# Half of one dense token tile's gates by scatter, two choices to a column; v block by block into four buffers; 16 early rows

## The chip, the core and the metric

The kernel runs on one core of a Trainium2 chip. The metric is the device time of one execution in microseconds. Before the change it is 1724.55 us, the median of three runs (1724.57, 1723.10, 1724.55).

## What is computed

A decoder layer on 512 tokens (plus 16 learned meta tokens): a state-space branch and an mLSTM branch are merged, and the result goes through PEER, a mixer that picks experts by product keys. The change touches only PEER. Every token has 8 heads; a head picks 16 of 128 x 128 = 16384 experts, each of which is one row of `u_tab` and one of `v_tab`:

```python
def block(xb):
    q = (xb @ w_q).astype(f32).reshape(PEER_TOKEN_BLOCK, PEER_HEADS, 2, PEER_HALF)
    s = jnp.einsum('thid,hikd->thik', q, keys32)
    sv, si = lax.top_k(s, PEER_TOPK)
    ...
    cs, ci = lax.top_k(cand, PEER_TOPK)
    eidx = jnp.take_along_axis(cidx, ci, axis=-1)
    gate = jax.nn.softmax(cs, axis=-1)
    ug = u_tab[eidx]
    act = jax.nn.gelu(jnp.einsum('td,thkd->thk', xb, ug).astype(f32))
    vg = v_tab[eidx]
    return jnp.einsum('thk,thkd->td', (gate * act).astype(vg.dtype), vg)
```

After it the layer's input is added and a last norm is taken.

## The kernel before

Everything up to the PEER queries (`front`) takes about the first 475 us. In `peer` the 512 tokens are four tiles of 128.

**Tile 0 gathers.** Its 128 choices per token are 128 columns. For each column GpSimd fetches 128 rows of u by an indirect DMA (`fetch`), VectorE multiplies with the tokens and sums (`use`, L1142), and later 128 rows of v are fetched and added into `ac0` (L1150). Of these 256 rows `NEARLY` = 25 are fetched before the main loop (tiles `ge`), the rest in it (tiles `g`).

**Tiles 1 to 3 are dense.** The experts are 128 blocks j of 128. `hidden(j)` computes u-block times tokens: 8 x 3 TensorE products (the float32 operand is split by ScalarE and VectorE into a high part `uh` and a low part `ul`, and three of the four partial products are taken, L84, L87 and L88) and a GELU, which gives `act`. In the main loop each block j forms `w` = gates x `act`, splits it (`wh`, `wl`), splits v's block (`vh`, `vl`) and adds 18 products of 128x512 to the three output tiles `o`. Each engine's instructions stand in one order, and each is begun in that order.

**Hidden blocks ahead of the loop.** `NSP` = 44 pairs of blocks (88 blocks) are computed in the stages before the loop, written to DRAM (`ad`) and read back in the loop (`act<-ad`); `LEFT` = 8 blocks are computed last before the loop and stay on chip; the other 32 are computed in the loop, six blocks ahead of their use (`RA`).

**Gates.** Dense gates are a matrix of 16384 experts by 384 tokens, mostly zeros. Tiles 2 and 3 make theirs by one-hot matrices (`gates`): for 8 tokens at a time VectorE builds `o` (L1045, one compare) and `ow` (L1045, one multiply), TensorE multiplies them token by token into `gp` (L1486), ScalarE copies them out to `stg` (L1488), and each 32 tokens are a block of 2 MB that is written to `gd`. Tile 1 scatters: `pairs_of` computes an address for each of the 128 x 128 choices (`ix`), and `scatter` lets GpSimd add one column of 128 gates at a time into `gds`, a DRAM array that `front` has filled with zeros by 8 DMAs. A head's 16 columns follow the head before. The last 32 tokens of tile 3 have their u rows gathered too (`NSIDE` = 32 rows `ge<-in_u,xsi`, L1349 and L1357).

**What sets the order.** In the gate stage `beside` paces GpSimd: six scatters, then three early rows, by a clock that counts TensorE's work; a row's VectorE instruction is put into the program when it is due, `LAG` after its slot. `fill` spreads the hidden blocks over the stage. Tile 1's and 3's pairs and those of tile 0 come first, those of tile 2 beside the gates. The early rows lie in the buffers of v (`vraw`, two of 1 MB, each a pair of blocks). In the loop SyncE's one queue issues all plain loads: v by pairs, u by pairs, `act`, and `gin` (gates of 8 blocks, from `gds` and `gd`). A load waits in that queue until its buffer is free, and what stands behind it waits too.

Of the kernel before, what the change touches and what calls it, by code (L numbers as in the profile page):

```python
# [11 lines left out]
F32 = mybir.dt.float32  # L12
# [3 lines left out]
I32 = mybir.dt.int32  # L16
# [35 lines left out]
JB = 8  # L52
PAR = (("g1", 8), ("a_re", 16), ("a_im", 16), ("log_dt", 16), ("b_glu", 4), ("conv_w", 32), ("conv_b", 8),
# [11 lines left out]
def tile_hybrid_block(ctx: ExitStack, tc: tile.TileContext, a: dict, out: bass.AP, dbg: dict | None = None):  # L65
# [55 lines left out]
    gds = dram.tile([P, NKEY // JB, P // TB, JB, TB], F32, name="gds")  # L121
# [8 lines left out]
def front(tc, a, dbg, cst, dram, xnp, ident, h2d, xsd, gds, x0, qt01, dump, split, mm3, rsqrt, rsqrt_cols):  # L130
# [3 lines left out]
    with es:  # L134
# [63 lines left out]
        blank = [x for x in gds.rearrange("i g b j t -> (i g b j t)").rearrange("(n p c d) -> n p c d", n=8, p=P, d=D)]  # L198
# [825 lines left out]
def peer(tc, a, out, dbg, cst, dram, xh, xl, blanks, ident, h2d, xsd, gds, x0, qt01, dump, split, mm3, rsqrt_cols):  # L1024
# [9 lines left out]
    NSP = 44  # L1034
# [3 lines left out]
    NEARLY = 25  # L1038
# [3 lines left out]
    GS = 32768.0  # L1042

# [4 lines left out]
    with es:  # L1048
# [3 lines left out]
        gd = dram.tile([2 * P // TB, P, NKEY, TB], F32, name="gd")  # L1052
# [175 lines left out]
        def pairs_of(i, h0=0, h1=PH):  # L1228
# [3 lines left out]
            if h0 == 0:  # L1232
                prs[i] = [pw.tile([P, PH, TOPK], F32, tag=t, name=f"{t}{i}") for t in ("cs", "ef")]
                prs[i].append(pool.tile([P, P], F32, name="gw1") if i == 1 else w0 if i == 0 else
                              pw.tile([P, P], F32, tag="gw", name=f"gw{i}"))
                if i == 1:
                    prs[i].append(pool.tile([P, P], I32, name="ix1"))
                if i == NT - 1:
                    prs[i].append(pw.tile([P, P], F32, tag="er", name="er", bufs=1))
# [66 lines left out]
            if i == 1:  # L1306
                ix = prs[i][3].rearrange("p (h k) -> p h k", h=PH)[:, hs]
                off = pw.tile([P, nh, TOPK], F32, tag="off", name=f"off{n_}", bufs=1)
                V.tensor_copy(ix, ef)
                V.tensor_scalar(ix, ix, JB - 1, None, op0=OP.bitwise_and)  # L1310
                V.tensor_copy(off, ix)
                V.tensor_scalar(ef, ef, float(P), cpf[:, 0:1], op0=OP.mult, op1=OP.add)
                V.scalar_tensor_tensor(ef, off, float(TB - P), ef, op0=OP.mult, op1=OP.add)
                V.tensor_copy(ix, ef)
                cols.extend((prs[i][3], prs[i][2], c) for c in range(h0 * TOPK, h1 * TOPK))
# [5 lines left out]
        RB = 3  # L1321
        NE = 6
        C0 = 24
        LAG = 18.0
        early = dict(t=8.0, columns=0, due=[], got=0, used=0, may=0, jk=None, last=None)
# [43 lines left out]
        def beside(flush=False):  # L1369


            e, total = early, NSIDE + NEARLY
            while True:
# [6 lines left out]
                if e["t"] > t or not cols and e["got"] == total:  # L1380
                    break
                n = min(RB, e["may"] - e["got"], NE - (e["got"] - e["used"]))
                if n > 0 and (not cols or e["columns"] % 6 == 0 and e["got"] < (e["columns"] - C0) // 6 * RB):
                    for n in range(e["got"], e["got"] + n):
                        k = n % NE
                        if k < 4:
                            if k % 2 == 0:
                                e["two"] = up.tile([P, 2, D], F32, tag="vraw", name=f"ge{n}", bufs=2)
                            r = e["two"][:, k % 2]
                        else:  # L1390
                            r = rw.tile([P, D], F32, tag=f"early{k}", name=f"ge{n}", bufs=1)
                        e["last"] = tc.keep_in_program_order(fetch_early(n, r))
                        e["t"] += 1.65
                        e["due"].append(e["t"] + LAG + 2.0 * (n % RB))
                        e["got"] += 1
                elif cols:
                    scatter(1)
                    e["t"] += 2.2 if e["columns"] % TOPK else 4.0
                else:
                    break  # L1400

        def scatter(n):

            early["columns"] += len(cols[:n])
            for ix, wt, c in cols[:n]:
# [4 lines left out]
                h = c // TOPK  # L1410
                if c % TOPK == 0:
                    heads.append([])
# [18 lines left out]
        def gates(i, others, blocks):  # L1431
# [33 lines left out]
            for b in blocks:  # L1465
                stg = rw.tile([P, NKEY, TB], F32, tag="stg", name=f"stg{i}{b}")
                for q in range(TB // 8):
# [23 lines left out]
                    fill(1.35 + 0.68 * np_)  # L1491
                    next(others, None)
                    next(others, None)
                SY.dma_start(gd[(i - 2) * (P // TB) + b], stg)
# [16 lines left out]
        whole = 4 * 24 + 2 * 16 * 2.75 + NSIDE * 1.3 + 6  # L1511
# [15 lines left out]
        def beside_gates():  # L1527
            yield from filled(2)

# [13 lines left out]
        for of in ((1, PH // 2, PH), (3,), (0,)):  # L1543
            for _ in filled(*of):
                pass
            if of == (3,):
                placed(prs[NT - 1][3], 3)
                spread()
                early["jk"] = True
                early["may"] = NSIDE  # L1550
            if of == (0,):
                placed(prs[0][1].rearrange("p h k -> p (h k)"), 0)
                V.tensor_copy(e0, prs[0][1].rearrange("p h k -> p (h k)"))
                early["may"] = NSIDE + NEARLY
        rest = beside_gates()
        gates(3, rest, range(P // TB - 1))
        gates(2, rest, range(P // TB))
        assert early["used"] >= NSIDE, early
# [32 lines left out]
        def added(i, c, eng=None):  # L1591

            y, x = hr[i][:, cc[c]], op_[i - 1] if i else ac0
            if sq[i] is None:
                two = up.tile([P, 2, D], F32, tag="vraw", name=f"sq3{i}", bufs=2)
# [173 lines left out]
```

## Time and profile before

| | |
|---|---|
| time, three runs | 1724.57, 1723.10, 1724.55 us |
| profiled execution | 1725.33 us, its span 1723.3 us |
| TensorE | 1634.4 us busy, 95% of the span |
| VectorE, ScalarE, GpSimd | 1307.8, 703.2, 755.3 us busy |
| mean granted TensorE clock | 0.979 |
| bytes moved | 427.51 MB, mean 248 GB/s |

The profile is of one execution. A row of groups gives line, engine, operation, tiles written and read, count, then busy time and mean ns. A row of windows gives the stretch, its length, the busy time (with count) of TensorE's products, its weight loads, VectorE, ScalarE and GpSimd, the granted clock, the DMA engines' busy share and GB/s. A row of waits gives who waited for whom: total, times, longest. Busy time of TensorE counts a product from its start to its modelled end, so products that follow each other overlap; its real pace is read from start to start.

### The profile page before, as it was taken

How to read it: one execution, taken by the hardware profiler on the slowest of the kernel's cores; microseconds unless marked ns; L12 is line 12 of the kernel's file. 1: busy time of each engine (PE TensorE's matmuls, PEld its weight loads, DVE VectorE, ACT ScalarE, POOL GpSimd, SP SyncE). 2: the span in 40 equal slices, each digit the busy share in tenths (PEclk: the TensorE clock that was granted, in tenths of full speed). 3: DMA queues.
4: the chain of work that ended last, by engine and by line, in shares of the span. 5: the costliest groups of instructions: out<-in, count | busy, mean ns of one | idle time of the engine just before them, and what ended most of it. 6: DMA issues, size and time to landing. Idle time of an engine off the chain costs nothing.

```text
span 1723.3 us, 25271 instructions
## 1 busy us (share of the span) xinstructions
PE 1634.4 (95%) x9437; PEld 1426.9 (83%) x9437; DVE 1307.8 (76%) x2621; ACT 703.2 (41%) x1151; POOL 755.3 (44%) x506
## 2 busy tenths in 40 slices
PE   7999999999999999999999939999999989999997
PEld 7898787778889899988999928887888877777785
DVE  6996723366578899885687748887888877887986
ACT  4544454433233244544465613333333423333333
POOL 2000032232132778687887634343335645554640
PEclk9999999999999999999999969999999999999999
DMA  4514353114433367788989899999999989898983
GB/s 174 124 58 102 113 194 123 50 61 161 178 126 131 67 165 246 241 284 281 289 284 303 317 338 364 379 380 371 382 372 383 365 344 346 328 354 329 350 330 136
DMA packets 143427, 427.51 MB, mean 248 GB/s; under 512 B 42020, under 2 KB 58532, under 8 KB 125768
## 3 DMA queue, kind: packets, MB, share of 16 engines
q1 hardware_dynamic: 77048, 267.32, 43.3%
q0 software_dynamic: 59968, 151.09, 25.4%
q10 hardware_dynamic: 6288, 7.49, 1.3%
q8 instruction: 74, 1.21, 0.3%
q14 instruction: 49, 0.40, 0.1%
HBM read 378.29 MB, written 47.55 MB: 247 GB/s over the span
## 4 chain that ended last, share of the span: by engine, by line
PE 58%; DMA 17%; DVE 14%; issue 5%; POOL 3%; ACT 2%; ACTq 0%; DVEq 0%; POOLq 0%; SPq 0%
DMA v<-in_v 13%; PE h L84 5%; PE h L88 5%; PE h L87 5%; PE o L88 4%; PE o L87 4%; PE o L84 4%; DVE g L1142 3%; DVE ac L1150 2%; POOL gds L1406 2%; DVE vl L81 2%; PE q L87 2%; PE q L88 2%; PE q L84 2%; DMA ge<-in_u,xsi 1%
## 5 line engine op out<-in xcount | busy, mean ns | idle before, releaser
L84 PE MATMUL h<-x2h,uh 128*128 128x352 f32 x1024 | 336.2, 328 | 1.7 <-ACT act L1098 1.7
L88 PE MATMUL h<-x2h,ul 128*128 128x352 f32 x1024 | 333.6, 326 | 3.7 <-DVE ul L81 3.5
L87 PE MATMUL h<-x2l,uh 128*128 128x352 f32 x1024 | 332.2, 324 | 0.0
L84 PE MATMUL o<-vh,wh 128*128 128x512 f32 x768 | 275.7, 397 | 46.7 <-ACT vh L80 46.5
L1135 POOL DMA_INDIRECT g<-in_v,e x128 | 207.0, 1617 | 174.1 <-DVE ac L1150 159.3
L87 PE MATMUL o<-vl,wh 128*128 128x512 f32 x768 | 275.5, 397 | 1.8 <-DVE vl L81 1.8
L88 PE MATMUL o<-vh,wl 128*128 128x512 f32 x768 | 269.7, 397 | 3.9 <-DVE wl L1660 3.6
L1406 POOL DMA_INDIRECT gds<-gw,ix x128 | 244.3, 1909 | 58.8 <-issue 37.0
L81 DVE TENSOR_TENSOR vl<-v,vh 128x1024 fp32r<-128x1024 f32 x128 | 155.9, 1218 | 110.9 <-ACT vh L80 110.9
L80 ACT ACTIVATE uh<-u 128x1024 fp32r<-128x1024 f32 x128 | 135.5, 1062 | 208.5 <-PE h L87 166.2
L84 PEld LDWEIGHTS o<-vh,wh 128*128 128x128 f32 x768 | 145.4, 191 | 76.5 <-ACT vh L80 49.6
L84 PEld LDWEIGHTS h<-x2h,uh 128*128 128x128 f32 x1024 | 194.3, 190 | 5.1 <-ACT act L1098 2.6
L88 PEld LDWEIGHTS h<-x2h,ul 128*128 128x128 f32 x1024 | 193.4, 189 | 5.8 <-DVE ul L81 4.4
L87 PEld LDWEIGHTS h<-x2l,uh 128*128 128x128 f32 x1024 | 193.9, 189 | 1.5
L1135 POOL DMA_INDIRECT g<-in_u,e x103 | 113.4, 1101 | 184.7 <-DVE g L1142 176.6
L88 PEld LDWEIGHTS o<-vh,wl 128*128 128x128 f32 x768 | 145.7, 190 | 46.7 <-DVE wl L1660 16.7
L80 ACT ACTIVATE vh<-v 128x1024 fp32r<-128x1024 f32 x128 | 131.4, 1054 | 113.6 <-DMA v<-in_v 71.8
L87 PEld LDWEIGHTS o<-vl,wh 128*128 128x128 f32 x768 | 146.0, 191 | 35.9 <-DVE vl L81 5.7
L81 DVE TENSOR_TENSOR ul<-u,uh 128x1024 fp32r<-128x1024 f32 x128 | 155.4, 1217 | 23.3 <-ACT uh L80 23.1
L1645 ACT ACTIVATE wh<-w 128x384 fp32r<-128x384 f32 x128 | 67.0, 523 | 253.3 <-DVE w L1640 253.2
L1150 DVE SCALAR_TENSOR_TENSOR ac<-g,w,ac 128x1024 f32<-128x1024 f32 x127 | 162.1, 1276 | 0.0
L1142 DVE SCALAR_TENSOR_TENSOR g<-g,x 128x1024 f32<-128x1024 f32 x103 | 125.2, 1216 | 0.0
(540 smaller groups left out, 3028.2 us busy)
## 6 DMA issues: line engine op xcount, KB each, us to landing
u<-in_ut SPq DMA_DIRECT2D x64, 1024.0 KB, 6.9
v<-in_v SPq DMA_DIRECT2D x64, 1024.0 KB, 12.9
gd<-stg SPq DMA_DIRECT2D x8, 2048.0 KB, 11.4
gi<-gd SPq DMA_DIRECT2D x16, 1024.0 KB, 14.8
ad<-act SPq DMA_DIRECT2D x44, 352.0 KB, 4.4
act<-ad SPq DMA_DIRECT2D x44, 352.0 KB, 9.3
gds<-qt SPq DMA_DIRECT2D x8, 1024.0 KB, 5.2
gi<-gds SPq DMA_DIRECT2D x16, 512.0 KB, 8.6
```

The lines of the kernel that those rows point to most:

```text
L80: A.activation(hi, src, AF.Copy)
L81: return eng.tensor_tensor(lo, src, f32(hi), op=OP.subtract)
L84: i_ = PE.matmul(ps, lh, rh, start=first, stop=False)
L87: PE.matmul(ps, lh, rl, start=False, stop=False)
L88: return PE.matmul(ps, ll, rh, start=False, stop=last)
L1135: return GP.indirect_dma_start(out=t, out_offset=None, in_=a["u"] if s_ < P else a["v"], in_offset=bass.IndirectOffsetOnAxis(ap=e0[:, c:c ...
L1142: i_ = V.scalar_tensor_tensor(g, g, 1.0, x0, op0=OP.mult, op1=OP.mult, accum_out=hsl[:, c:c + 1])
L1150: i_ = V.scalar_tensor_tensor(ac0, g, w0[:, c:c + 1], ac0, op0=OP.mult, op1=OP.add)
L1406: i_ = GP.indirect_dma_start(out=gds.rearrange("i g b j t -> (i g b j t)").unsqueeze(1), out_offset=bass.IndirectOffsetOnAxis(ap=ix[:, c:c ...
L1645: A.activation(wh, w, AF.Copy)
```

## The change

Of tile 1 only the first `HP` = 64 tokens are scattered; the other two blocks of 32 go through `gates(1, ...)` as one-hot matrices. A scatter column now holds two choices of each of 64 tokens: choices 0 to 7 of a head stand on partitions 0 to 63, choices 8 to 15 are moved to partitions 64 to 127 by a TensorE product with the identity. So there are 64 scatters of 128 gates, 8 to a head, `gds` has half the size and 4 DMAs fill it, and `gd` has 10 blocks. v is loaded block by block into four buffers of 512 KB. `NSP` falls from 44 to 38, `NEARLY` from 25 to 16. `beside` alternates one scatter and one row; `LAG` is 22. Tile 0's pairs move from ahead of the gates to beside them, behind tile 2's, and all early rows are used up ahead of the leftover hidden blocks.

```diff
+HB = 2
+HP = HB * TB
-    gds = dram.tile([P, NKEY // JB, P // TB, JB, TB], F32, name="gds")
+    gds = dram.tile([P, NKEY // JB, HB, JB, TB], F32, name="gds")
...
-    NSP = 44
+    NSP = 38
-    NEARLY = 25
+    NEARLY = 16
...
-        gd = dram.tile([2 * P // TB, P, NKEY, TB], F32, name="gd")
+        gd = dram.tile([NTD * P // TB - HB, P, NKEY, TB], F32, name="gd")
...
+                p = mp.tile([P, 2, nh, CH_], F32, tag="tr", name=f"xp{n_}")
+                for n, x in enumerate((off, w)):
+                    PE.matmul(p[HP:, n], ident[:, :HP], x[:, :, CH_:], start=True, stop=True)
+                for o, x, n in ((ix, off, 0), (cw, w, 1)):
+                    V.tensor_copy(o[:HP], x[:HP, :, :CH_])
+                    V.tensor_copy(o[HP:], p[HP:, n])
...
-        LAG = 18.0
+        LAG = 22.0
...
-                n = min(RB, e["may"] - e["got"], NE - (e["got"] - e["used"]))
-                if n > 0 and (not cols or e["columns"] % 6 == 0 and e["got"] < (e["columns"] - C0) // 6 * RB):
+                e["t"] = max(e["t"], clock[0] - 8.0)
+                if e["got"] < e["may"] and e["got"] - e["used"] < NE and (e["turn"] or not cols):
...
-                SY.dma_start(gd[(i - 2) * (P // TB) + b], stg)
+                SY.dma_start(gd[(i - 1) * (P // TB) + b - HB], stg)
...
-        for of in ((1, PH // 2, PH), (3,), (0,)):
+        for of in ((1, PH // 2, PH), (3,)):
...
+        def more():
+            yield from filled(2)
+            yield from filled(0)
+            placed(prs[0][1].rearrange("p h k -> p (h k)"), 0)
+            V.tensor_copy(e0, prs[0][1].rearrange("p h k -> p (h k)"))
+            early["may"] = NSIDE + NEARLY
+        rest = more()
         gates(3, rest, range(P // TB - 1))
+        gates(1, rest, range(HB, P // TB))
         gates(2, rest, range(P // TB))
...
         gates(3, rest, [P // TB - 1])
+        beside(True)
         for j, h in todo + [(j, h) for j in range(LEFT) for h in range(4)]:
             hidden(j, 2 * h, 2 * h + 2)
-            beside()
-        beside(True)
...
-            if j % 2 == 0:
-                vraw = up.tile([P, 2, D], F32, tag="vraw", name=f"v{j}", bufs=2)
-                SY.dma_start(vraw, a["v"][j * P:(j + 2) * P].rearrange("(p n) d -> p n d", n=2))
-            raw = vraw[:, j % 2]
+            raw = up.tile([P, D], F32, tag="vraw", name=f"v{j}", bufs=4)
+            SY.dma_start(raw, a["v"][j // 2 * 2 * P:(j // 2 + 1) * 2 * P].rearrange("(p n) d -> p n d", n=2)[:, j % 2])
```

**Where instructions move.** On SyncE's queue, at the end of the gate stage, before the change: `gd<-stg33` is the last gate block's write, `gi0` and `gi8` are the gates of the first 16 blocks, `v0` and `v2` the first pairs of v.

```order
L1494 DMA gd_4323<-stg33_9580 128x4096
L1630 DMA gi0_10017<-gds_67 128x1024
L1634 DMA gi0_10017<-gd_4323 128x8x256
L1634 DMA gi8_10374<-gd_4323 128x8x256
L1638 DMA v0_10021<-in_v 128x2048
L1638 DMA v2_10092<-in_v 128x2048
```

After the change, on the same queue, the first blocks of v stand among the u loads of the gate stage (`stg20` is the first gate block of tile 2):

```order
L1500 DMA gd_4319<-stg20_8373 128x4096
L1639 DMA v0_9787<-in_v 128x1024
L1082 DMA u58_8905<-in_ut 128x2048
L1105 DMA ad_4320<-act55_8731 128x704
L1082 DMA u60_9019<-in_ut 128x2048
L1639 DMA v1_9821<-in_v 128x1024
L1639 DMA v2_9860<-in_v 128x1024
L1639 DMA v3_9897<-in_v 128x1024
```

So four blocks of v stand some twenty DMAs ahead of the first `gi`, where they stood behind the second `gi`.

On SyncE's queue in the loop, before the change, at blocks 74 to 78, pairs of v and a pair of u:

```order
L1638 DMA v72_13300<-in_v 128x2048
L1502 DMA act39_13294<-ad_4324 128x704
L1630 DMA gi72_13296<-gds_67 128x1024
L1079 DMA u46_13873<-in_ut 128x2048
L1502 DMA act40_13371<-ad_4324 128x704
L1634 DMA gi80_13653<-gd_4323 128x8x256
L1638 DMA v74_13374<-in_v 128x2048
```

And after it, at blocks 79 to 84:

```order
L1508 DMA act41_13546<-ad_4320 128x704
L1082 DMA u45_13914<-in_ut 128x2048
L1508 DMA act42_13622<-ad_4320 128x704
L1639 DMA v79_13662<-in_v 128x1024
L1639 DMA v80_13735<-in_v 128x1024
L1639 DMA v81_13802<-in_v 128x1024
L1639 DMA v82_13841<-in_v 128x1024
L1636 DMA gi88_14129<-gd_4319 128x10x256
L1639 DMA v83_13878<-in_v 128x1024
```

The large loads of u and of the gates no longer stand directly ahead of one large load of v; a block of v stands between them.

On GpSimd's queue in the gate stage, before and then after (`gds` are scatters, `ge` early rows):

```order
L1406 DMA gds_67<-gw1_4880,ix1_4881 2097152x1 x6
L1349 DMA ge6_6702<-in_u,xsi_4328 128x1024 x2
L1349 DMA ge8_6811<-in_u,xsi_4328 128x1024 x2
L1349 DMA ge10_6814<-in_u,xsi_4328 128x1024
L1349 DMA ge11_6931<-in_u,xsi_4328 128x1024
L1406 DMA gds_67<-gw1_4880,ix1_4881 2097152x1 x6
```

```order
L1412 DMA gds_67<-cw1_4878,ix1_4877 1048576x1
L1356 DMA ge5_6464<-in_u,xsi_4324 128x1024
L1412 DMA gds_67<-cw1_4878,ix1_4877 1048576x1
L1356 DMA ge6_6491<-in_u,xsi_4324 128x1024
L1412 DMA gds_67<-cw1_4878,ix1_4877 1048576x1
L1356 DMA ge7_6575<-in_u,xsi_4324 128x1024
```

Bursts have become single rows, each behind one scatter.

More of the change, by code (lines that the diff above doesn't have):

```diff
@@ L197, in front @@
         blanks = []
-        blank = [x for x in gds.rearrange("i g b j t -> (i g b j t)").rearrange("(n p c d) -> n p c d", n=8, p=P, d=D)]
+        blank = [x for x in gds.rearrange("i g b j t -> (i g b j t)").rearrange("(n p c d) -> n p c d", n=4, p=P, d=D)]
         p5 = ExitStack()
@@ L1306, in pairs_of @@
             if i == 1:
[L1307 to L1315, printed above, removed]
+                ix, cw = (x[:, hs] for x in prs[i][3:])
+                off = pw.tile([P, P], F32, tag="ej", name=f"off{n_}", bufs=1)[:, :nh * TOPK].rearrange("p (h k) -> p h k", h=nh)
+                oi = pw.tile([P, P], I32, tag="ei", name=f"oi{n_}", bufs=1)[:, :nh * TOPK].rearrange("p (h k) -> p h k", h=nh)
+                V.tensor_copy(oi, ef)
+                V.tensor_scalar(oi, oi, JB - 1, None, op0=OP.bitwise_and)
+                V.tensor_copy(off, oi)
+                V.tensor_scalar(off, off, float(TB * (HB // 2 - HB)), cpf[:, 0:1], op0=OP.mult, op1=OP.add)
+                V.scalar_tensor_tensor(off, ef, float(HP), off, op0=OP.mult, op1=OP.add)
+                p = mp.tile([P, 2, nh, CH_], F32, tag="tr", name=f"xp{n_}")
[4 more added lines that the diff above has]
+                    V.tensor_copy(o[HP:], p[HP:, n])
+                cols.extend((*(x.rearrange("p h k -> p (h k)") for x in prs[i][3:]), c) for c in range(h0 * CH_, h1 * CH_))
             yield 2.0
         cols = []
-        RB = 3
         NE = 6
-        C0 = 24
-        LAG = 18.0
-        early = dict(t=8.0, columns=0, due=[], got=0, used=0, may=0, jk=None, last=None)
+        LAG = 22.0
+        early = dict(t=8.0, columns=0, due=[], got=0, used=0, may=0, turn=0, last=None)
         def spread():
@@ L1369, in beside @@
         def beside(flush=False):
-            e, total = early, NSIDE + NEARLY
+            e = early
             while True:
@@ L1379, in beside @@
                     e["used"] += 1
-                if e["t"] > t or not cols and e["got"] == total:
+                if e["t"] > t:
                     break
-                n = min(RB, e["may"] - e["got"], NE - (e["got"] - e["used"]))
-                if n > 0 and (not cols or e["columns"] % 6 == 0 and e["got"] < (e["columns"] - C0) // 6 * RB):
[L1384 to L1395, printed above, removed]
+                e["t"] = max(e["t"], clock[0] - 8.0)
+                if e["got"] < e["may"] and e["got"] - e["used"] < NE and (e["turn"] or not cols):
+                    n, e["turn"] = e["got"], 0
+                    k = n % NE
+                    if k < 4:
+                        r = up.tile([P, D], F32, tag="vraw", name=f"ge{n}", bufs=4)
+                    else:
+                        r = rw.tile([P, D], F32, tag=f"early{k}", name=f"ge{n}", bufs=1)
+                    e["last"] = tc.keep_in_program_order(fetch_early(n, r))
+                    e["t"] += 1.65 if cols else 3.0
+                    e["due"].append(e["t"] + LAG)
+                    e["got"] += 1
                 elif cols:
                     scatter(1)
-                    e["t"] += 2.2 if e["columns"] % TOPK else 4.0
-                else:
+                    e["turn"] = 1
+                    e["t"] += 2.2 if e["columns"] % CH_ else 4.0
+                elif e["got"] == e["may"] or not flush:
                     break
```

37 lines of the change are left out of this document (14 added, 23 removed).

## Prediction

> **What bounds the kernel now.** I read the busy shares by slice first, then the long stretches by windows, then who ends TensorE's waits.
>
> ```profile
> PE   7999999999999999999999939999999989999997
> PEclk9999999999999999999999969999999999999999
> ```
>
> TensorE is busy nearly all the time from the fifth slice on, with one hole in the 24th of the 40 slices, where the granted clock falls too. So time can go only where TensorE does more or less work, where it idles, and where its clock is low. The windows split the part that the change touches: gate stage (from the last scores to the last gate product), hole, main loop.
>
> ```profile
> 596.00:985.00 389.00, 380.44 (x2668) 370.11 (x2667) 314.13 (x687) 198.12 (x251) 298.79 (x169) 0.99 0.83 267
> 985.00:1020.00 35.00, 5.17 (x41) 4.59 (x38) 10.52 (x20) 5.86 (x9) 12.83 (x11) 0.61 0.99 374
> 1020.00:1712.00 692.00, 668.47 (x3067) 557.92 (x3067) 579.84 (x771) 251.38 (x457) 313.45 (x224) 0.98 0.91 345
> ```
>
> For TensorE's real pace I take starts of rows from the timeline, 29 steps of hidden products apart and 22 steps of loop products apart, and 32 gate products from the chain.
>
> ```profile
> 924.90 0.32 PE L84 MATMUL h<-x2h,uh 128*128 128x352 f32 x1
> 929.58 0.32 PE L88 MATMUL h<-x2h,ul 128*128 128x352 f32 x1
> 1684.97 0.39 PE L84 MATMUL o<-vh,wh 128*128 128x512 f32 x1
> 1689.96 0.39 PE L84 MATMUL o<-vh,wh 128*128 128x512 f32 x1
> 949.11 1.86 PE gp L1486 x32
> ```
>
> 4.68/29 = 0.161 us for a hidden product, 4.99/22 = 0.227 for a loop product, 1.86/32 = 0.058 for a gate product. Now the counts, from windows of the tiles h and o:
>
> ```profile
> 596.00:985.00 389.00, 358.85 (x2116) 0.99 0.83 267
> 1020.00:1712.00 692.00, 131.72 (x764) 0.98 0.91 345
> 1020.00:1712.00 692.00, 553.50 (x2303) 0.98 0.91 345
> ```
>
> Gate stage: 2116 x 0.161 + 512 gate products x 0.058 + about 1 for the transposes = 372 us of 389; 17 are lost. Loop: 764 x 0.161 + 2304 x 0.227 = 646 us of 692; **46 are lost**. In the loop TensorE's waits are these:
>
> ```profile
> PE o L84 <- ACT vh L80: 17.7, 6, 5.3
> PE o L88 <- DVE wl L1660: 3.6, 6, 0.7
> ```
>
> They and small ones make 23 us; the other half is the clock after such a wait, as in the first window here against the second. The chain shows why vh is late: a pair of v takes 22.85 us from issue to landing, with a 1 MB load of u issued just ahead of it.
>
> ```profile
> 1400.00:1420.00 20.00, 14.65 (x62) 11.76 (x62) 8.42 (x10) 5.33 (x11) 3.90 (x4) 0.91 0.88 347
> 1360.00:1380.00 20.00, 20.00 (x98) 17.21 (x97) 16.53 (x20) 9.17 (x16) 11.45 (x7) 1.00 1.02 415
> 1392.60 0.33 SPq L1079 DMA_DIRECT2D u<-in_ut  x1
> 1394.17 22.85 DMA v<-in_v
> v<-in_v SPq DMA_DIRECT2D x64, 1024.0 KB, 12.9
> ```
>
> With two buffers of a pair, a pair's load starts when the pair two before it is split, and is wanted one pair later: 2 x 5.4 = 10.8 us (692/128 = 5.4 a block). A median landing of 12.9 is more than that. So the loop is bound by TensorE with v's ring of buffers close behind; VectorE (580 of 692) is not far.
>
> **The change, part by part.** The profiled execution took 1725.33 us (span 1723.3), 0.8 above the median of the runs.
>
> *Hidden blocks.* Six pairs fewer ahead of the loop: 12 blocks x 24 = 288 products go from before the loop into it. By the order of instructions 30 of them leave the scores stage (-4.8 us, TensorE full there) and 282 the gate stage (24 of these move only behind the last gate product, into the hole): -45.5 us. The loop gets 288: **+46.5 us**. Their six u loads go along, and six writes and readings of `ad` vanish.
>
> *One-hot blocks.* Two more blocks of 64 products: 128 x 0.058 = 7.4, with four transposes and four small products about **+8.2 us** of TensorE. The gate stage's work is thus 389 - 45.5 + 8.2 = 352 us if it loses 17 again.
>
> *Can VectorE feed that?* It gets 8 `o` and 8 `ow` more, and 11 `ul` fewer:
>
> ```profile
> L1045 DVE TENSOR_TENSOR ow<-o,wb 128x2048 f16<-128x2048 f16 x28 | 34.0, 1217 | 0.3
> L81 DVE TENSOR_TENSOR ul<-u,uh 128x1024 fp32r<-128x1024 f32 x88 | 106.9, 1218 | 23.3 <-ACT uh L80 23.1
> ```
>
> (16 - 11) x 1.22 = 6, and some ten small copies and casts: 314 + 7 = 321 us busy. Busy time and waits fill the stage now (314 + 73 = 387 of 389). In 352 there is room for 31 us of waits; now there are 73:
>
> ```profile
> DVE ge L1357 <- DMA ge<-in_u,xsi: 30.0, 7, 9.8
> DVE ul L81 <- ACT uh L80: 23.1, 16, 3.7
> DVE ge L1142 <- DMA ge<-in_u,e: 13.0, 5, 7.9
> DVE o L1045 <- PE gp L1486: 6.1, 6, 2.0
> ```
>
> The second and fourth are waits on TensorE's pace and shrink when VectorE has no spare time. The first and third, 43 us, are rows that land after they are due, and behind each stand the `ul` and `ow` that TensorE needs. After the change a row is due 22 us behind its slot, not 18, rows no longer come in threes behind six scatters, and the pacing no longer lags. I take 10 us of them; the bounds are 0 and 43. GpSimd itself issues 64 scatters fewer:
>
> ```profile
> L1406 POOL DMA_INDIRECT gds<-gw,ix x128 | 244.3, 1909 | 58.8 <-issue 37.0
> ```
>
> 64 x 1.91 = 122 us less, off the path except through those rows. Half the zeros of `gds` go as well; TensorE is full in that stage, so that is worth nothing.
>
> *The hole.* Now: the last gates are written, read back, and v comes last.
>
> ```profile
> 987.62 0.33 SPq L1494 DMA_DIRECT2D gd<-stg  x1
> 1001.01 32.17 SPq L1638 DMA_DIRECT2D v<-in_v  x4
> 1011.44 0.34 ACT L1642 COPY w<-gi 128x32 f32<-128x32 f32 x2 [21.22 <-DMA gi<-gd]
> 1012.13 0.52 ACT L1645 ACTIVATE wh<-w 128x384 fp32r<-128x384 f32 x1 [0.35 <-DVE w L1640]
> 1018.56 2.00 ACT L80 ACTIVATE vh<-v 128x1024 fp32r<-128x1024 f32 x2 [5.91 <-DMA v<-in_v]
> 1019.67 1.65 PE o L84 x3
> ```
>
> v0 waits for the early rows that lie in its buffers, is issued at 1001.01 and landed at 1018.5. After the change v0 to v3 stand far ahead of the gates. What is late next is `gi`: wh would be done at 1012.65, so the loop starts 25 us behind the last write, not 32: **-7 us**. `gi0` reads more (ten blocks of `gd`, 1.25 MB for 1 MB), but 4 MB of v are no longer beside it; between 0 (gi as much later) and -14 (gi in half its 15 us) I stay at -7.
>
> *v by blocks.* In a ring of four, block j+4 starts when block j is split and is wanted four blocks later: 4 x 5.5 = 22 us, against the 10.8 above. The landing of 512 KB in this queue isn't shown; its bounds are the rows of 512 KB loads in a quieter stage and of the pair above, 22.85 at worst.
>
> ```profile
> wq<-in_w_q SPq DMA_DIRECT2D x14, 512.0 KB, 4.0
> g<-in_v,e POOLq DMA_INDIRECT x128, 8.7
> ```
>
> I take about 9, like the gathered rows (also 512 KB) in the same loop. Then v is late only behind a burst at its worst. Of the 46 us lost in the loop I keep 14: about 5 for wl and vl, 4 for the slow clock at either end, 5 for such bursts. Bounds: 0 and 46. Against it, the Trainium skill ("DMA: Bandwidth & Descriptors", section "Rules for kernel authors") asks for at least 1 MiB in each DMA; here each v load falls to half of that. No row of this loop shows a 512 KB plain load; what the rule would make of the sum is the rival on DMA rate below.
>
> *Nine rows* move into the loop: 9 x 1.2 on VectorE, which has 112 us idle there, and 4.7 MB. No cost on TensorE.
>
> The sum: scores -4.8; gate stage -45.5 + 8.2 = -37.3; hole -7; loop +46.5 - 32 = +14.5. Together -34.6: 1725.3 - 34.6 = 1690.7, and 0.8 less beside the median: **1690 us**.
>
> **Rivals.**
>
> *VectorE becomes the bound of the gate stage* (slower). For it: 321 of 352 us busy, and by the order of instructions VectorE's and TensorE's sums run level through the whole stage, so a late row stalls TensorE at once. If all 73 us of waits stay, the stage takes 321 + 73 = 394, +5 for -37.3: 1732. It decides from 66 us of waits on; against it, 29 of the 73 give way by themselves. Chance 0.10.
>
> *v stays late:* the blocks split one burst into two, but all stand in the same queue behind the same u and `gi`. Then the loop keeps its 46 us: +46.5 in place of +14.5, 1722, no change. Against it are the 22 us of lead. Chance 0.13.
>
> *The DMA engines bind the loop.* Up to the tail it moves this:
>
> ```profile
> 1020.00:1680.00 660.00, 637.02 (x2932) 532.62 (x2932) 556.18 (x730) 237.65 (x427) 313.45 (x224) 0.98 0.93 355
> ```
>
> 355 GB/s x 660 us = 234.3 MB. Added are 12 blocks of u (6.3 MB) and nine rows (4.7), gone 12 blocks of `act` (2.2): 243.1 MB. At the pace forecast, 674 us, that is 361 GB/s; 20 us windows reached 415. At 347 GB/s, the rate of the stalled window above, it takes 701: +41, 1716. The skill's page gives 341 GB/s for 1 MB DMAs and less below (section "Bandwidth"); by that, worked out as an estimate, 243.1/341 = 713 us and about 1728. The 415 speak against it. Chance 0.12.
>
> *Everything gives way:* no late rows, no v stalls: some 16 us better, 1674. Chance 0.05.
>
> **How the numbers follow.** The forecast of 1690 has 0.60 and runs from about 1678 to 1705. The range goes down to 1670 for the last rival and up to 1720, which takes in the DMA rival; outside are the first rival, most of the second and a few hundredths below. A measurement of this kernel tells about 0.2% (3.4 us) from no change. Faster: 0.60 + 0.05 + 0.12 and a third of the second rival, 0.81. The same: 0.08. Slower: 0.11.
>
> **What would show it.** Right: the last gate product about 42 us earlier, at 943; VectorE's waits on `ge` rows near 10; the first loop product about 25 us behind the last `gd` write, with `gi` as its releaser; a loop of about 706 us with few waits on vh and a clock of 0.99. Wrong: waits on `ge` over 40 us with TensorE idle behind VectorE; v landing 20 us after issue with vh still the releaser; or a loop at a DMA share near 1 with GB/s under 350.

## The result and the profile after

| | before | changed |
|---|---|---|
| median | 1724.49 us, 4 runs | **1697.46 us**, 4 runs (1693.28 to 1699.09) |
| ratio, 95% interval | | 0.9841 [0.9823, 0.9860] |
| profiled execution | 1725.33, span 1723.3 | 1693.28, span 1691.6 |

The change is faster by 1.6%. The forecast was 1690, the range 1670 to 1720. The profiled execution of the changed kernel is the fastest of its four; the median lies 4.2 us above it, so what is read from its trace is a little better than the usual run.

The page of the changed kernel, busy tenths of TensorE and its clock in 40 slices:

```profile
PE   7999999999999999988999899999999999999997
PEclk9999999999999999989999999999999999999998
```

The 3 in the 24th slice has gone: the hole now lies in the 23rd, which holds an 8. The 18th and 19th slices, in the gate stage, hold an 8 each that was not there. The windows of the same trace, by stage: gate stage, hole, loop (columns as in the prediction: busy PE, PEld, DVE, ACT, POOL with counts, clock, DMA share, GB/s).

```profile
593.00:957.00 364.00, 348.10 (x2537) 338.64 (x2536) 319.29 (x703) 196.83 (x246) 181.84 (x102) 0.98 0.79 275
957.00:974.00 17.00, 7.61 (x46) 7.02 (x45) 1.01 (x2) 7.82 (x12) 4.72 (x5) 0.86 0.89 317
974.00:1680.00 706.00, 698.52 (x3355) 602.74 (x3356) 603.84 (x801) 267.19 (x480) 320.69 (x236) 1.00 0.94 356
```

For all kernels below I cut at the starts of four rows of the timeline: the last scores product, the last gate product, the first and the last loop product. "Lost" is a stage less its work, at the prediction's 0.161, 0.227 and 0.058 us a product.

| | before, us | changed, us | difference | predicted |
|---|---|---|---|---|
| start to last scores product | 594.5 | 591.7 | -2.9 | -4.8 |
| gate stage | 391.2 | 365.0 | -26.2 | -37.3 |
| hole | 33.9 | 17.5 | -16.4 | -7 |
| loop | 692.5 | 705.9 | +13.4 | +14.5 |
| behind the last loop product | 11.1 | 11.5 | +0.4 | 0 |
| span | 1723.3 | 1691.6 | -31.7 | -34.6 |

Two terms are off by some 10 us, against each other: that the sum came within 3 us is luck.

The waits of VectorE in the gate stage of the changed kernel, then those of TensorE:

```profile
DVE ul L83 <- ACT uh L82: 14.5, 9, 5.4
DVE o L1048 <- PE gp L1492: 12.2, 8, 4.0
DVE ge L1364 <- DMA ge<-in_u,xsi: 9.5, 2, 7.0
DVE ge L1145 <- DMA ge<-in_u,e: 1.4, 1, 1.4
```

```profile
PE h L90 <- DVE ul L83: 6.4, 4, 2.9
PE gp L1492 <- DVE ow L1048: 4.9, 4, 2.2
PE h L86 <- ACT uh L82: 4.0, 2, 2.5
```

In the kernel before, TensorE's waits there were these:

```profile
PE gp L1486 <- DVE ow L1045: 4.2, 1, 4.2
PE h L88 <- DVE ul L81: 3.5, 1, 3.5
```

The waits on rows fell from 43 to 10.9 us, as taken, and yet TensorE waits 15.3 us on three lines where it waited 7.7. One place shows how, in the chain and in VectorE's timeline:

```profile
730.77 11.39 DMA ge<-in_u,xsi
```

```profile
742.19 1.22 DVE L1364 SCALAR_TENSOR_TENSOR ge<-ge,qt 128x1024 f32<-128x1024 f32 x1 [7.04 <-DMA ge<-in_u,xsi]
```

A row is issued at 730.77 and lands 11.4 us later; VectorE has reached it at 735.1 and stands for 7 us, with the next `ul` behind it. In the 15 us window that begins where the row lands, TensorE is busy for 9.85 us, at a clock of 0.77:

```profile
742.00:757.00 15.00, 9.85 (x73) 9.18 (x74) 13.21 (x22) 6.16 (x8) 12.56 (x9) 0.77 0.93 310
```

The chain through the hole (start, us, what; the longer pieces):

```profile
958.47 7.81 DMA gd<-stg
966.30 6.67 DMA gi<-gd
...
974.19 1.65 PE o L86 x3
```

The issue of `gi` in the kernel before, from SyncE's queue:

```profile
996.20 1.00 SPq L1634 DMA_DIRECT2D gi<-gd  x2
```

`gi` is the releaser, as forecast, but it lands in 6.7 us and not in 15.2 (issued 996.20, waited for until 1011.44 before). From the last `gd` write to the first loop product it is 15.7 us; 25 were forecast, 32 stood there before.

The waits of TensorE in the loop, and v's row among the DMA issues of the page (count, KB each, median us to landing):

```profile
PE o L86 <- ACT wh L1645: 6.5, 5, 1.6
PE o L89 <- DVE vl L83: 0.8, 1, 0.8
```

```profile
v<-in_v SPq DMA_DIRECT2D x128, 512.0 KB, 9.1
```

TensorE no longer waits on vh, and the landing of 9.1 us is the 9 that was taken. That looks like a proof that the ring of four blocks cured the loop. The experiments show a second cause that does as much without it.

### The profile page after: what moved, and what is told of

The parts are those of the page before. It is cut to its first block, busy times and chain, and to the rows that moved or that the text cites. A ratio compares the mean times of both kernels' runs of the same rounds, so it can differ in the third digit from the quotient of the medians.

```text
span 1691.6 us, 25682 instructions
## 1 busy us (share of the span) xinstructions
PE 1630.2 (96%) x9575; PEld 1438.0 (85%) x9575; DVE 1328.8 (79%) x2651; ACT 717.3 (42%) x1167; POOL 636.0 (38%) x442
## 4 chain that ended last, share of the span: by engine, by line
PE 85%; DVE 8%; DMA 3%; issue 2%; ACT 1%; POOL 1%; ACTq 0%; POOLq 0%; DVEq 0%
PE o L86 10%; PE o L89 10%; PE o L90 10%; PE h L90 8%; PE h L86 8%; PE h L89 8%; PE gp L1492 1%; PE q L90 1%; PE q L89 1%; PE q L86 1%; PE s L877 1%; PE n L886 1%; PE gm L377 1%; PE gm L380 1%; DVE ul L83 1%
## 5 line engine op out<-in xcount | busy, mean ns | idle before, releaser
L86 PE MATMUL o<-vh,wh 128*128 128x512 f32 x768 | 282.1, 393 | 15.1 <-ACT wh L1645 15.1
L89 PE MATMUL o<-vl,wh 128*128 128x512 f32 x768 | 281.1, 391 | 0.8 <-DVE vl L83 0.8
L1138 POOL DMA_INDIRECT g<-in_v,e x128 | 199.2, 1556 | 154.4 <-DVE ac L1153 144.2
L1138 POOL DMA_INDIRECT g<-in_u,e x112 | 126.2, 1127 | 281.1 <-DVE g L1145 176.5
L82 ACT ACTIVATE vh<-v 128x1024 fp32r<-128x1024 f32 x128 | 135.1, 1057 | 143.0 <-PE o L90 124.6
L83 DVE TENSOR_TENSOR ul<-u,uh 128x1024 fp32r<-128x1024 f32 x128 | 155.5, 1217 | 15.1 <-ACT uh L82 14.5
L1412 POOL DMA_INDIRECT gds<-cw,ix x64 | 127.0, 1984 | 42.1 <-issue 29.2
L1145 DVE SCALAR_TENSOR_TENSOR g<-g,x 128x1024 f32<-128x1024 f32 x112 | 135.9, 1213 | 0.5 <-DMA g<-in_u,e 0.5
```

What stands on the lines that cost most here:

```text
L82: A.activation(hi, src, AF.Copy)
L83: return eng.tensor_tensor(lo, src, f32(hi), op=OP.subtract)
L86: i_ = PE.matmul(ps, lh, rh, start=first, stop=False)
L89: PE.matmul(ps, lh, rl, start=False, stop=False)
L1138: return GP.indirect_dma_start(out=t, out_offset=None, in_=a["u"] if s_ < P else a["v"], in_offset=bass.IndirectOffsetOnAxis(ap=e0[:, c:c ...
L1145: i_ = V.scalar_tensor_tensor(g, g, 1.0, x0, op0=OP.mult, op1=OP.mult, accum_out=hsl[:, c:c + 1])
```

## The experiments

Two questions: what single parts of the change are worth by themselves, above all v's ring; and why the gate stage loses 31 us (365.0 less 1837 x 0.161 + 640 x 0.058 + 1.5 = 334.4) where 17 were taken (the kernel before loses 19.5 by these cuts).

**1. v by pairs again, in the changed kernel.**

```diff
-            raw = up.tile([P, D], F32, tag="vraw", name=f"v{j}", bufs=4)
-            SY.dma_start(raw, a["v"][j // 2 * 2 * P:(j // 2 + 1) * 2 * P].rearrange("(p n) d -> p n d", n=2)[:, j % 2])
+            if j % 2 == 0:
+                vraw = up.tile([P, 2, D], F32, tag="vraw", name=f"v{j}", bufs=2)
+                SY.dma_start(vraw, a["v"][j * P:(j + 2) * P].rearrange("(p n) d -> p n d", n=2))
+            raw = vraw[:, j % 2]
```

The early rows and the last squares go back to halves of the same buffers, as before the change.

> The changed kernel, with v (and the early rows and the last squares in the same buffers) by pairs in two buffers of 1 MB again; all else as changed. Theory, the depth of v's ring pays: the loop loses about 46 us again in place of 14, TensorE waits 18 us or more on vh, a pair lands 12 to 23 us after its issue, and the whole takes 1697 + 32 = 1729 us (1720 to 1735). Rival, the loop is easier because of what else moved into it (more hidden products, so that each pair lasts longer: 5.5 us a block in place of 5.4, with the same DMA rate): the loop loses about 14 us still and the whole stays at 1697 (within 4).

1704.59 us, ratio to before 0.9885 [0.9847, 0.9922]. The loop, by windows, and TensorE's longest waits in it:

```profile
982.00:1691.00 709.00, 701.65 (x3356) 602.34 (x3356) 604.84 (x802) 266.25 (x480) 317.76 (x236) 1.00 0.93 355
```

```profile
PE o L86 <- ACT vh L82: 4.5, 2, 2.4
```

For the loop the rival was right: it takes 708.2 us, 2.3 more than with blocks. The whole is 7 us longer, past the rival's 4; in the profiled executions 7.6 us lie in the gate stage (372.6), whose early rows lie in the same buffers. The pairs land sooner than before the change, 10.5 us in place of a median of 12.9, and so just within a lead of two blocks (2 x 5.5 = 11):

```profile
v<-in_v SPq DMA_DIRECT2D x64, 1024.0 KB, 10.5
```

**2. Blocks of v alone, in the kernel before**, with the early rows and the last squares in the same four buffers.

```diff
-            if j % 2 == 0:
-                vraw = up.tile([P, 2, D], F32, tag="vraw", name=f"v{j}", bufs=2)
...
+            raw = up.tile([P, D], F32, tag="vraw", name=f"v{j}", bufs=4)
```

> The kernel before, with one part of the change alone: v (and the early rows) by single blocks of 512 KB in four buffers. Theory: its loop falls from 692 to about 660 us, the waits of TensorE on vh from 17.7 to under 5, and the whole goes from 1724 to 1692 us (1688 to 1698), so that this part alone gives as much as the whole change. Rival, small loads are no better here (512 KB in each DMA moves fewer GB/s, or the same queue lands them as late): 1724 or slower. A third result, 1705 to 1715, would mean that the DMA engines, at 355 to 370 GB/s, bind this shorter loop.

1693.38 us, 0.9827 [0.9798, 0.9856]: as much as the whole change. Gate stage 392.9 and hole 34.4 stay; the loop falls from 692.5 to 658.9.

```profile
1022.00:1681.00 659.00, 652.89 (x3068) 555.32 (x3067) 579.19 (x771) 252.72 (x455) 312.62 (x224) 1.00 0.96 364
```

So the blocks are worth 33.6 us in the old loop and 2.3 in the new one. That is no contradiction if pairs cost only where the loop asks for nearly all that the DMA engines move. The next runs test it.

**3. Pairs of hidden blocks: 44 again in the changed kernel.**

```diff
-    NSP = 38
+    NSP = 44
```

> The changed kernel with 44 in place of 38 pairs of hidden blocks ahead of the loop, as before the change; all else as changed. Theory: the gate stage of the changed kernel lost 31 us in place of 17 because VectorE (320 us busy and 11 of waits on rows in 365) had no room left, so moving 282 products back costs less there than they save in the loop: loop 707 - 46.5 = 660, gate stage 365 + 45.5 - 14 = 397, the whole 1682 to 1686 us. Rival, the 31 us are lost to single late rows and bursts whatever TensorE has to do: gate stage 411, the whole 1696. Second rival: the loop shortened to 660 is bound by the DMA engines and gives back 10 us or more: 1694 or above.

1704.53 us, 0.9887 [0.9857, 0.9917]. Only the second rival's "1694 or above" takes it in, because both rivals hold at once. The loop takes 668.1 us, 22 lost, and the gate stage 415.5, 39 lost (2096 x 0.161 + 640 x 0.058 + 1.5 = 376).

```profile
595.00:1010.00 415.00, 391.45 (x2800) 380.97 (x2799) 334.52 (x714) 213.91 (x267) 178.25 (x101) 0.97 0.75 258
...
1026.00:1694.00 668.00, 656.48 (x3068) 557.28 (x3068) 589.58 (x789) 250.44 (x454) 316.32 (x235) 0.99 0.97 370
```

That VectorE lacked room in the changed kernel's gate stage falls with this: here it has 80 us of room (334.5 busy of 415), and more is lost. In the loop the second rival shows: at 370 GB/s and a DMA share of 0.97 the engines give no more.

**4. The order of the last rows undone.**

```diff
-        beside(True)
         for j, h in todo + [(j, h) for j in range(LEFT) for h in range(4)]:
             hidden(j, 2 * h, 2 * h + 2)
+            beside()
+        beside(True)
```

> The changed kernel with the last early rows used between and behind the leftover hidden blocks, as before the change, and not ahead of them; all else as changed. Theory, the hole went from 32 to 16 us because v0 to v3 are loaded ahead of the last gates, so that gi travels alone (6.7 us in place of 15): here v waits for the rows' buffers again, gi lands in 10 us or more, and the whole takes 1704 to 1713 us. Rival, the rows are done in time in any order, because 16 of them end earlier than 25 did and the pacing no longer lags: no change, 1697 (within 3).

1698.77 us, 0.9862 [0.9832, 0.9891]: no change; hole 17.7. With 16 rows nothing is left there to be ordered.

**5. 38 pairs of hidden blocks alone, in the kernel before.**

```diff
-    NSP = 44
+    NSP = 38
```

> The kernel before, with one part of the change alone: 38 pairs of hidden blocks ahead of the loop in place of 44; v still by pairs of 1 MB. Before, the loop asked the DMA engines for 238.7 MB in 646 us of TensorE work, 369 GB/s, and lost 46 us; the changed kernel with pairs of v asked 363 and lost 14. Theory, pairs of v cost time only where the loop asks for nearly what the DMA engines move: here the loop takes 706 to 712 us (14 to 20 lost), the gate stage 346 to 360, and the whole 1692 to 1708. Rival, the 46 us belong to the pairs and stay whatever the loop asks for: loop 738, whole 1725 to 1738.

1738.28 us, 1.0082 [1.0053, 1.0110]: slower. Half of the theory held. The loop, with pairs of v, takes 702.2 us and loses 10, less than the 14 to 20 it named. But the hole is 67.4 us (gate stage, hole, loop):

```profile
592.00:954.00 362.00, 339.94 (x2412) 331.51 (x2411) 294.70 (x667) 181.37 (x228) 263.36 (x149) 0.97 0.79 253
954.00:1021.00 67.00, 5.23 (x32) 4.65 (x30) 17.67 (x30) 5.95 (x11) 41.87 (x33) 0.55 0.78 264
1021.00:1723.00 702.00, 699.52 (x3355) 601.85 (x3356) 594.70 (x783) 267.87 (x481) 309.84 (x224) 1.00 0.91 345
```

GpSimd's groups within that hole (count, busy and mean ns, idle):

```profile
L1406 POOL DMA_INDIRECT gds<-gw,ix x14 | 23.2, 1658 | 4.3 <-issue 4.3
L1135 POOL DMA_INDIRECT ge<-in_u,e x12 | 12.1, 1010 | 3.7 <-issue 3.4 <-DMA gds<-gw,ix 0.3
```

In a gate stage of 362 us GpSimd doesn't get through its 128 scatters and 57 rows: it is busy for 263 us, and the rest goes between issues and into waits for scatters to land and for buffers of rows. 14 and 12 are left, and the loop waits for both, through `gi` and through the buffers of v. TensorE's loss in the gate stage is 35 us, of which 21 are this wait, and all but 0.8 us of it ends within some 5 us behind a row that VectorE had to wait for:

```profile
PE h L88 <- DVE ul L81: 21.3, 5, 9.6
```

GpSimd, off the path before, becomes the bound of the hole as soon as the work that covers it moves away.

**6. The changed kernel with 44 pairs and v by pairs** (the edits of runs 1 and 3).

```diff
-    NSP = 38
+    NSP = 44
...
-            raw = up.tile([P, D], F32, tag="vraw", name=f"v{j}", bufs=4)
+                vraw = up.tile([P, 2, D], F32, tag="vraw", name=f"v{j}", bufs=2)
```

> The changed kernel with two parts undone: 44 pairs of hidden blocks ahead of the loop, and v by pairs of 1 MB in two buffers. With blocks this loop asked for 247 MB in 646 us (383 GB/s), moved 370 GB/s and took 668. Theory, pairs cost most where the loop asks for more than the DMA engines move: the loop takes 695 to 715 us, the whole 1732 to 1755. Rival, what made pairs harmless in the changed kernel is not what the loop asks for but the early load of v0 to v3 or the smaller gds: loop near 668 to 672, whole 1705 to 1712 (the gate stage takes up to 8 us more with pairs).

1738.33 us, 1.0081 [1.0051, 1.0110], as the theory had it. The loop takes 711.8 us, 66 lost, and TensorE waits for v; the window, and the wait:

```profile
1014.00:1725.00 711.00, 673.99 (x3065) 558.85 (x3065) 589.36 (x789) 249.57 (x452) 315.04 (x234) 0.97 0.91 347
```

```profile
PE o L86 <- ACT vh L82: 29.1, 9, 6.5
```

**7. Blocks, and 16 early rows ahead of the leftover blocks, in the kernel before** (on top of run 2).

```diff
-    NEARLY = 25
+    NEARLY = 16
...
+        beside(True)
         for j, h in todo + [(j, h) for j in range(LEFT) for h in range(4)]:
             hidden(j, 2 * h, 2 * h + 2)
-            beside()
-        beside(True)
```

> The kernel before with v and the early rows by single blocks in four buffers (1693.4 us by itself, hole 34, loop 659), and 16 in place of 25 rows of token tile 0 early, all rows used ahead of the leftover hidden blocks. Scatters, one-hot blocks and 44 pairs stay as before. Theory, the hole is long because rows of the 25 are still open when the last gates are written, and v0 to v3 wait for their buffers and then travel beside gi: hole 16 to 20 us in place of 34, loop 659 + 9 for 4.7 MB more through engines that are full, whole 1680 to 1690. Rival, the 128 scatters keep the rows late and 9 rows less change nothing: hole 30 or more, whole 1695 to 1705.

1688.18 us, 0.9785 [0.9760, 0.9810], as the theory had it: hole 15.9, loop 670.0.

```profile
1009.00:1679.00 670.00, 657.12 (x3068) 557.84 (x3067) 589.12 (x789) 251.18 (x454) 319.11 (x235) 0.99 0.97 369
```

The DMA engines are full again, as in run 3, and 24 us are lost (22 there). Against run 2, nine rows more in the loop cost it 11 us, and TensorE's waits on `wh` went from 5.2 to 11.1.

**8. The same with 38 pairs**: the changed kernel without its scatters, one-hot blocks, place of tile 0's pairs and pacing of rows.

```diff
-    NSP = 44
+    NSP = 38
```

> As the kernel before with blocks of v and 16 early rows ahead of the leftover blocks, and also 38 pairs of hidden blocks: the changed kernel without its new scatters, its two more one-hot blocks and its new order and pacing of rows. Theory, the gate stage of the changed kernel lost 31 us in place of 17 because of what is new in it there: here it loses 17 (391 - 45.5 = 346 us, 340 to 352), loop 706, hole 16 to 20, the whole 1668 to 1680. Rival, any gate stage with 282 hidden products less uncovers VectorE and late rows: 355 to 365 us, the whole 1685 to 1697, as the changed kernel.

1714.19 us, 0.9929 [0.9904, 0.9954], above both. The gate stage takes 361.5 us, so the theory (what is new in it causes the loss) falls: it loses 35 without any of it. What neither had is the hole of 35.2: GpSimd again, with 12 scatters left.

```profile
L1404 POOL DMA_INDIRECT gds<-gw,ix x12 | 20.7, 1727 | 3.7 <-issue 3.0 <-DMA gds<-gw,ix 0.6
```

**9. Early rows due later in the changed kernel.**

```diff
-        LAG = 22.0
+        LAG = 30.0
```

> The changed kernel with an early row due on VectorE 30 us behind its slot in place of 22; nothing else. Open is why the gate stage lost 31 us and not 17. Theory, single late rows: VectorE stood 7 us on one row at 735 to 742 us and TensorE stood behind it; with 8 us more the waits on rows fall from 11 to 2 us or less, the gate stage from 365 to 357 to 360, the whole to 1690 to 1693. Rival, VectorE's own work is crowded into the first part of the stage (14 to 15 us busy of each 15 from 592 to 710 and from 757 to 877, 10 behind 892): the gate stage stays at 363 to 367, the whole at 1697 (within 3). Second rival, the last rows end later and the hole grows by 5 us or more: 1700 or above.

1681.13 us, 0.9749 [0.9716, 0.9782]: the lowest time of all, with an interval that lies wholly below the changed kernel's (run 10, at 1682.34, isn't told apart from it). The gate stage takes 351.8 us, with the same work for VectorE:

```profile
593.00:944.00 351.00, 340.22 (x2527) 333.35 (x2526) 317.86 (x702) 196.42 (x245) 188.60 (x102) 0.99 0.82 284
```

Its waits there:

```profile
DVE ge L1364 <- DMA ge<-in_u,xsi: 14.8, 5, 4.3
DVE o L1048 <- PE gp L1492: 6.9, 4, 3.2
DVE ul L83 <- ACT uh L82: 5.5, 8, 1.1
```

The theory's size is passed (351.8 for 357 to 360), but not by its own sign: the waits on rows did not fall to 2, they rose to 14.8. What fell is the longest (7.0 to 4.3), the waits of VectorE on what TensorE and ScalarE have yet to free (26.7 to 12.4), and TensorE's loss at a low clock. Of the 13.2 us that the stage gained, TensorE idles 5 less (15.9 to 10.8 by the windows), 2 are 12 products that moved behind the last gate, and some 6 are products that follow each other closer, with a mean clock of 0.99 for 0.98.

**10. Rows due later in the version of run 7.**

```diff
-        LAG = 18.0
+        LAG = 30.0
```

> The kernel before with blocks of v and 16 early rows ahead of the leftover blocks (1688.2 us by itself; gate stage 397, of which 25 are lost, VectorE 56 us waiting for rows), with rows due 30 us behind their slot in place of 18. Theory, late rows make the loss: VectorE's waits on rows fall under 25 us, the gate stage to 382 to 390, the whole to 1672 to 1681. Rival, the rows are held back by GpSimd, which has 128 scatters to issue between them, and the slots slip as well: waits on rows 40 or more, gate stage 394 or more, the whole 1685 to 1692. Second rival, the rows that end later meet the last gates, and the hole grows from 16 towards 34.

1682.34 us, 0.9754 [0.9721, 0.9787], 1.3 above the theory's bounds. The gate stage falls from 397.1 to 386.2 and loses 14; VectorE waits 19.6 us on rows in place of 56. The hole is 20.8.

```profile
DVE ul L81 <- ACT uh L80: 29.3, 22, 4.2
DVE o L1045 <- PE gp L1484: 19.8, 12, 4.3
DVE ge L1357 <- DMA ge<-in_u,xsi: 12.5, 3, 7.5
DVE ge L1142 <- DMA ge<-in_u,e: 7.1, 1, 7.1
```

Here VectorE waits for the others and not they for it: the spare time that a stage paced by TensorE shows.

**11. 8 early rows in the changed kernel.**

```diff
-    NEARLY = 16
+    NEARLY = 8
```

> The changed kernel with 8 in place of 16 rows of token tile 0 early. Theory, VectorE's sum sets the gate stage: 8 x 1.2 = 10 us less work there, gate stage 354 to 358; in the loop 4.2 MB more, 255.7 MB for 692 us of work, 369 GB/s, which with blocks lost 13 us in the kernel before: loop 706 to 710, the whole 1687 to 1693. Rival, the loss lies in the first half of the stage, where the rows are those of the side tokens and not of tile 0: gate stage 362 to 366, the whole 1695 to 1702.

1706.45 us, 0.9894 [0.9855, 0.9934]. 10 us less work for VectorE change nothing in the gate stage (366.6), so the rival holds there. The loop takes 717.1 us, 25 lost: more than either had.

```profile
976.00:1693.00 717.00, 702.65 (x3355) 605.08 (x3356) 612.92 (x817) 267.01 (x479) 334.43 (x243) 0.99 0.95 356
```

VectorE has 16 instructions more there than in the changed kernel (817 for 801), and the DMA engines 4 MB; TensorE's waits on `wh` go from 6.5 to 13.5 us. The eight rows that leave the gate stage cost this loop 11 us.

**12. Rows due still later in the changed kernel.**

```diff
-        LAG = 22.0
+        LAG = 36.0
```

> The changed kernel with an early row due 36 us behind its slot (22 as changed, 30 in the version of 1681.1 us). By the order of instructions 10 of the 48 early rows now stand behind the last gates on VectorE, as 11 did in the kernel before; none did with 22 or 30. Theory, it is those rows that made the hole 34 us: v0 to v3 wait for their buffers and then travel beside gi, so the hole is 28 to 36 us again, the gate stage 340 to 352 (less of VectorE's work in it), the whole 1688 to 1700. Rival, the hole was shortened by something else (half of gds, two blocks of gd more), and rows used behind the last gates fit beside the way of gi: hole 17 to 21, gate stage 340 to 350, the whole 1668 to 1682, a better version still.

1687.63 us (1681.43 to 1693.24), 0.9774 [0.9739, 0.9808]; the profiled execution is the slowest of the four. Gate stage 341.9, hole 39.5: a hole past the theory's 28 to 36, and a time at its lower bound, since 127 hidden products in place of 46 now lie in the hole. The last steps into the loop on VectorE:

```profile
947.25 1.23 DVE L1145 SCALAR_TENSOR_TENSOR ge<-ge,x 128x1024 f32<-128x1024 f32 x1 [5.51 <-DMA ge<-in_u,e]
...
972.71 0.53 DVE L1640 TENSOR_TENSOR w<-gi,act 128x352 f32<-128x352 f32 x1 [20.81 <-DMA gi<-gd]
```

And SyncE's queue in that hole:

```profile
936.20 0.32 SPq L1500 DMA_DIRECT2D gd<-stg  x1
936.61 3.12 SPq L1639 DMA_DIRECT2D v<-in_v  x2
939.82 1.28 SPq L1082 DMA_DIRECT2D u<-in_ut  x1
941.19 2.32 SPq L1639 DMA_DIRECT2D v<-in_v  x2
950.78 0.33 SPq L1082 DMA_DIRECT2D u<-in_ut  x1
951.34 0.33 SPq L1632 DMA_DIRECT2D gi<-gds  x1
951.72 0.42 SPq L1636 DMA_DIRECT2D gi<-gd  x1
```

v0 to v3 are issued only behind the last write of `gd`. `gi` is issued 15.5 us behind that write (7.8 in the changed kernel), because a u load ahead of it in the queue isn't issued until 950.78, and it travels 20.9 us among them. That u load waits for the `ul` behind the late row of 947.25, and the chain that ended last goes from that row through the load and `gi` into the loop. The 127 hidden products, 20 us of work, stand beside that chain and not on it.

## Why the prediction was right, and where it was not

**The loop: right by 1 us, in part by luck.** The step said that the lead of the ring, 22 us in place of 10.8, takes 32 of 46 lost us away. In the old loop blocks do that (run 2), but in the changed one they aren't needed: run 1 has the short lead and loses 16. Of the 14 us that the sum kept, the total came out and the parts didn't: TensorE waits 0.8 us on vl and wl, where about 5 were taken, and 6.5 on wh, which wasn't named. All loops side by side; MB is GB/s by the length of the loop's window, divided by the loop's work (646 us with 764 hidden products, 692 with 1052) for what it asks of the DMA engines:

| kernel | v by | MB | asked, GB/s | loop, us | lost |
|---|---|---|---|---|---|
| run 5 | pairs | 242 | 350 | 702.2 | 10 |
| run 1 | pairs | 252 | 364 | 708.2 | 16 |
| before | pairs | 239 | 369 | 692.5 | 46 |
| run 6 | pairs | 247 | 382 | 711.8 | 66 |
| changed | blocks | 251 | 363 | 705.9 | 14 |
| run 8 | blocks | 251 | 363 | 711.8 | 19 |
| run 11 | blocks | 255 | 369 | 717.1 | 25 |
| run 2 | blocks | 240 | 371 | 658.9 | 13 |
| runs 3, 7 | blocks | 247 | 383 | 668.1, 670.0 | 22, 24 |

With pairs the loss climbs steeply between 364 and 369 GB/s; with blocks it stays between 13 and 25. Both loops with pairs below that step have 38 pairs of hidden blocks ahead, both above it 44, so the table doesn't separate the rate asked from whatever else that shift changes in the loop. What it does to v is in the rows: a pair lands in 10.5 us in run 1 and in 12.9 in the kernel before, with a lead of 11 and of 10.8. The change does two things, each of which alone would have taken away some 30 us (run 2: 33.6; run 5: from 46 lost to 10), and both together take 32. In the changed kernel the hidden blocks that moved in give TensorE more work for each byte, and the blocks of v add 2.3 us. Whether the blocks help by their size or by the number of buffers was not separated either. Why run 11 loses more than run 2 at the same figure stays open.

The rival on the DMA rate was priced on a wrong reading: 347 GB/s is what the engines moved while the ring stalled, not what they can move. Runs 3 and 7 hold 370 and 369 GB/s over a whole loop. The Trainium skill ("DMA: Bandwidth & Descriptors", section "Rules for kernel authors") asks for at least 1 MiB in each DMA; the old loop moved the same bytes at 345 GB/s with v loads of 1 MB and at 364 with those of 512 KB (run 2), so the measurement decides against the rule in this loop, where the larger load leaves a ring half as many places.

**The gate stage: the term was mis-sized by 11 us.** The step that failed is "352 us if it loses 17 again": it lost 31. The waits on rows came as taken (10.9 for 10), and the work too. But a gate stage with 282 products less lost 30 to 38 us in runs 1, 4, 5, 8 and the changed kernel, with old and new scatters alike (rows due at 18 or 22 us). The first rival's direction was right, its measure wrong: not the sum of VectorE's waits decides (run 9 waits longer on rows and is 13 us faster; run 3 has room and loses 39), nor its work (run 11). What the traces point to is whether a row that is late stands in VectorE's queue ahead of an `ul` or `ow` that TensorE needs next: so it is with nearly all of TensorE's 21 us of waits in run 5. In the changed kernel only 5 of its 15.9 idle us stand right behind a late row (to 718 and to 745 us); another 7 follow up to 799, and 3 at 883 to 886 have no late row ahead of them. So for this kernel the cause is in part argued. With rows 8 us later the stage takes 351.8, the forecast's 352. Whether the later place of rows in VectorE's order helps by itself, or only through the shorter waits, was not separated; small changes in the rows' buffers also move this stage by 8 to 14 us in either direction (run 1 against the changed kernel, run 6 against run 3).

**The hole: mis-sized on the good side.** -16.4 for -7, past the end of the bound of -14. The step "between 0 and -14 I stay at -7" took `gi`'s 15.2 us as its own; they were the company's. With no load of v ahead of it or close behind `gi` lands in 6.7 us, behind and beside four blocks of v and two loads of u in 20.9 (run 12). Sixteen rows in place of 25, used ahead of the leftover blocks, are enough for it (run 7); in the changed kernel that order adds nothing (run 4).

**Scores: -2.9 for -4.8.** Run 4, with the same 30 products fewer, reaches the last scores product at 593.3 and run 9 at 591.5: the 1.9 us that are missing are no more than two such executions differ by.

**What the prediction costed at nothing.** The scatters were put off the path "except through those rows". In the changed kernel that holds, but only because they were halved: without that the same shift of hidden blocks ends in a hole of 67 us (run 5) or 35 (run 8). The nine rows, too, were given "No cost on TensorE". For these nine in the changed loop no run shows it, but nine rows more cost the old loop with blocks 11 us (run 7 against run 2), and eight more cost the changed loop 11 (run 11).

From 1714.2 to 1697.5 us the scatters, one-hot blocks, order and pacing pay 16.7; with 44 pairs, where the longer stage covers GpSimd, the same parts cost 16 (1688.2 in run 7, 1704.5 in run 3).

So the 27 us are not a sum of parts. The blocks of v would have done as much by themselves (1693.4), and more with 16 rows (1688.2). With rows due 30 us behind their slot the changed kernel takes 1681.1 us, and the version with the old scatters and 44 pairs takes 1682.3 (run 10): beside the blocks of v, the 16 rows and their due time, the scatters, one-hot blocks and the shift of hidden blocks show no gain that the intervals tell apart.

## What to carry to other kernels

Before a stall in a loop is put down to a ring's depth, divide the bytes that the loop moves by the work of the engine that paces it: near the rate that the DMA engines reached, smaller blocks in more buffers and more work for each byte each cured the same stall here, and they didn't add up. Work moved out of a stage uncovers whoever worked unseen beside it, so count what the quietest engine still has to issue there before the stage gets shorter. And a landing time in a crowded queue belongs to the crowd: ask what it would be alone before it is carried over.

## What the runs showed of the hardware that was not expected

The DMA engines held 370 GB/s for 668 us (run 3). The Trainium skill gives some 358 GB/s, half of what a memory stack delivers to its two cores, as one core's limit ("DMA: Bandwidth & Descriptors", section "Specifications"). This kernel runs on one core, and its loops at 364 to 370 show that for it the figure is no ceiling.

A stall of TensorE costs more than its length. In the kernel before, the 46 us that the loop lost can be added up from the starts of its products: 23.5 are idle; some 16 lie in 88 products that took more than 1.3 times their usual step, three quarters of them within 6.5 us behind a wait; some 5 are the ends of the last products before the 28 gaps, which nothing overlaps; 2 are the rest. Behind the longest wait three products start 0.48 us apart in place of 0.227, and the clock is 0.50:

```profile
1418.22 1.65 PE L84 MATMUL o<-vh,wh 128*128 128x512 f32 x3 [5.35 <-ACT vh L80]
1418.00:1422.00 4.00, 3.78 (x8) 2.45 (x9) 3.80 (x4) 1.22 (x3) 1.01 (x1) 0.50 0.04 14
```

Much shorter waits did the same: behind one of 2.2 us the clock was 0.50 from 1512 to 1514 us. So the prediction read its "other half" of the 46 rightly, as the clock after the waits. In the changed kernel's gate stage the 31 lost us are 15.9 idle, some 10 in slow steps and some 2 in ends before a wait; the last few are in the estimate of the work.
